# Attention scores of two heads on 64 rows each instead of stacked on 128 rows

## The chip, the cores and the metric

One core of a Trainium2 chip runs the whole program. The metric is the device time of one execution in microseconds (us); lower is better. The names of the engines are those of the profile: PE is TensorE (matmuls, with PEld for its weight loads), DVE is VectorE, ACT is ScalarE, POOL is GpSimd, SP is SyncE, which issues the DMAs.

## What is computed

The reference is a decoder trunk of two layers over 512 tokens of width 1024, in float32. Each layer is a half-step SwiGLU, a token mixer, and a second half-step SwiGLU, each modulated by vectors of c and closed by a post-norm:

```python
for l in range(DEPTH):                                   # DEPTH = 2
    y = _swiglu(_modulate(x, sh1, sc1), ...);  x = _post_norm(x, y, g1, FFN_RES, ...)
    y = _token_mixer(_modulate(x, sh2, sc2), w_in[l], w_out[l]);  x = _post_norm(x, y, g2, 1.0, ...)
    y = _swiglu(_modulate(x, sh3, sc3), ...);  x = _post_norm(x, y, g3, FFN_RES, ...)
```

The change is in the token mixer. It projects its input to ten blocks and runs three groups of four heads: retention, dilated softmax attention, and stick-breaking attention. Two of them need scores of queries with keys over a head width of 64:

```python
z  = einsum('bhqd,bhsd->bhqs', q_blk * d**-0.5, k)       # stick-breaking, no positions, strictly causal
sc = einsum('bhqd,bhqpjd->bhqpj', q_blk * d**-0.5, k_g)  # dilated windows, q and k rotated before
```

The kernel computes the dilated scores against all keys of the causal range and adds the logarithm of how often a pattern holds each key.

## The kernel before

**Split products.** A matrix product of two float32 operands is made of float32r parts: each operand is split into an upper part `hi` and the rest `lo`, and PE adds up hi·hi, hi·lo and lo·hi in PSUM (`mm3`, L180 to L183). For weights, `unit` (L167) loads a piece of 512 KB into a raw tile, ACT writes `hi` (L176), DVE writes `lo` (L177). The products of the projections are the lines L181, L182, L183 in every table.

**The mixer.** `mixer` (L504) first makes the projections `sv` and `sq`. The other projections are generators (`jobs`). The attentions (`stick` L675, `dilated` L740, `retention` L788) are generators too: at each `yield` they hand over a number of microseconds of PE work, which `fill` takes from the projections and puts in between. So the order on PE is a score product, some projection products, the next dependent product of an attention, and so on. A scheduler fixes the final order of each engine before the program runs, and every engine then works through its own list in that order.

**Heads by pairs.** The projections of q and k come out transposed, [128, 512 tokens] for a pair of heads: head a = 0 stands in rows 0 to 63, head a = 1 in rows 64 to 127 (`hsl(a)`). Before, `stack_q` and `stack_k` make a stacked copy of 128 rows for each head: for q, the upper part on the head's own 64 rows and the lower part on the other 64; for k, the upper part on both halves, and the lower parts in a tile of their own (`sklo`, `dklo`). One product over 128 rows then gives hi·hi + hi·lo of one head, and one product over 64 rows gives lo·hi. A score call (`scores_T` for stick, `scores_q` for dilated) makes four matmuls: full, 64 rows, full, 64 rows (L615 and L616, L628 and L629), with a PSUM bank per head. There are 8 calls per attention and layer, with 256, 256, 384 and 512 columns for each of the two pairs.

**Stick-breaking.** A step takes the scores, makes `sb_w` (absolute value, exp, log on ACT: L700, L703, L704), `sb_sp` (DVE L706, POOL L708), its parts `sb_hi` (ACT L711) and `sb_lo` (DVE L712). PE sums those over the keys (L722, L723 for the block itself; L727, L728 for later blocks). The scores of step n + 1 are issued on PE between the scores of step n and L722 of step n.

**Dilated.** The scores are scaled and masked (DVE L750), the maximum is taken (L752), exp on ACT (L755), the division on DVE (L756, L758) into `d_sc`; PE transposes it (L770), ACT copies it out (L773), PE multiplies it with the values (L780). The scores of step n + 1 stand ahead of the transposes of step n.

**Rotation.** q and k of the dilated heads go through `rotate` (L643) ahead of the stacking: four copies on ACT (L650), DVE L651, POOL L652, DVE L653.

Of the kernel before, what the change touches and what calls it, by code (L numbers as in the profile page):

```python
# [10 lines left out]
F32 = mybir.dt.float32  # L11
F32R = mybir.dt.float32r
# [4 lines left out]
P = 128  # L17
D = 1024
T = 512
# [48 lines left out]
def trunk(ctx: ExitStack, tc: tile.TileContext, x_in, c_in, w_ada, b_ada, ln_gain, ln_bias,  # L68
# [18 lines left out]
    def big(shape, dt=F32, name="big"):  # L87
        return bigp.tile(shape, dt, tag="big", name=name)
# [145 lines left out]
    def chain(parts):  # L234
        """The steps of several vectors; what follows a sum over the partitions comes a few steps behind it."""
        u, late = [], None
        for steps, final in parts:
            if late is None:
                u += steps
            else:  # L240
                u += steps[:POST] + [late] + steps[POST:]
            late = final
        return u + [lambda: None] * POST + [late] if parts else u
# [51 lines left out]
    class PostNorm:  # L295
# [59 lines left out]
        def head(self):  # L355
            """The first token pair's part of the next input."""
            if self.h is not None:
                make_h(0, self.h, self.a, self.b)

        def rest(self):  # L360
            """The second token pair's part of the next input, and the residual stream."""
            ends = make_h(1, self.h, self.a, self.b)
            with tc.issue_after(self.last.ins):
                for t in range(NT):
                    G.tensor_tensor(out=xres[t], in0=xres[t], in1=self.gain, op=ALU.mult)
                    G.tensor_tensor(out=xres[t], in0=xres[t], in1=self.bias, op=ALU.add)
            return ends

# [28 lines left out]
    def gu_units(l, wg, wu, f, n, spare=False):  # L397
        """Units of gate and up for ff tiles f .. f+n-1, as (which, first k, units)."""
        us = []
        kn = 8 // n  # L400
        for wi, w in enumerate((wg, wu)):
            for k0 in range(0, KC, kn):
                us.append((wi, k0, kn, unit(w[l, k0 * P:(k0 + kn) * P, f * P:(f + n) * P]
                                            .rearrange("(k p) f -> p k f", p=P), (kn, n * P), spare)))
        return us

    REST_AT = 3       # unit of the first group after which the second token pair's input is made
    REST_AT_Q = 3     # the same in the mixer, by row chunks of the first projection
    LAST_CUT = (256, 256, 512, 1024)  # columns that VectorE finishes at the end, per token tile
    DRAIN = (3, 2)    # adaLN steps per group of gate and up, and per unit of down  # L410
    RES = 4           # units of down that stay for the token-major end
    ACT_HEADS = (1, 3)  # retention heads whose norm ScalarE applies
    OUT_EARLY = 2     # token tiles of the output projection begun beside retention
    # projections, in us of the tensor engine, put between the dependent parts of the attentions
# [62 lines left out]
    def hsl(a):  # L477
        return slice(a * HD, (a + 1) * HD)
# [4 lines left out]
    def pair_psum(N):  # L483
        """PSUM for two [P, N] blocks: views per block, and one view of both when they share a bank."""
        if fits(N):
            ps = psum()
            v = ps[:, 0:2 * N].rearrange("p (a n) -> p a n", a=2)
            return [v[:, 0, :], v[:, 1, :]], [(slice(0, 2), v)]
        b = [psum(), psum()]
        return [b[0][:, 0:N], b[1][:, 0:N]], [(a, b[a][:, 0:N]) for a in range(2)]  # L490

    class Packs:
        """[P, 2, N] tiles for N = 128, 256, 384, 512: 128 and 384 share a slot."""
# [10 lines left out]
    def mixer(l, h, pre, rest, prefetch, nxt):  # L504
        hh, hl = h
        yT = {}
        # -- projections, as generators that yield the time of what they gave to the tensor engine --
# [62 lines left out]
        def stack_q(name, m, src, scale=1.0):  # L570
            """[P, 2, T]: per head its rows' upper and lower parts, one part at the head's own rows."""
            r = big([P, 2, T], F32R, name)
            for a in range(2):
                o, x = hsl(a), hsl(1 - a)
                S.activation(out=r[o, a, :], in_=src[o, :], func=AF.Copy, scale=scale)
                V.scalar_tensor_tensor(out=r[x, a, :], in0=src[o, :], scalar=scale, in1=r[o, a, :].bitcast(F32),
                                       op0=ALU.mult, op1=ALU.subtract)
            val[name, m] = r

        def stack_k(name, m, src):  # L580
            """Per head its rows' upper parts twice, and the lower parts at the head's own rows."""
            r = big([P, 2, T], F32R, name)
            if m == 0:
                val[name, "lo"] = big([P, 2, T], F32R, name + "lo")
            lo = val[name, "lo"]
            for a in range(2):
                o, x = hsl(a), hsl(1 - a)
                S.copy(out=r[o, a, :], in_=src[o, :])
                V.tensor_copy(out=r[x, a, :], in_=r[o, a, :].bitcast(F32))
                V.tensor_tensor(out=lo[o, m, :], in0=src[o, :], in1=r[o, a, :].bitcast(F32), op=ALU.subtract)  # L590
            val[name, m] = r
# [7 lines left out]
        def wide(lo, hi):  # L599
            """At least 256 columns, the wanted ones within them."""  # L600
# [5 lines left out]

        def scores_T(kn, qn, pr, J):
            """Per head of pair pr, in banks apart: [keys of block J, queries >= 128 J]."""
            cs, v = wide(J * P, T)
            res = []  # L610
            for a in range(2):
                ps = psum()
                w = ps[:, 0:cs.stop - cs.start]
                js = slice(J * P, (J + 1) * P)
                PE.matmul(w, lhsT=val[kn, pr][:, a, js], rhs=val[qn, pr][:, a, cs], start=True, stop=False)  # L615
                PE.matmul(w, lhsT=val[kn, "lo"][hsl(a), pr, js], rhs=val[qn, pr][hsl(a), a, cs], start=False, stop=True)  # L616
                res.append(ps[:, v])
            return res

        def scores_q(qn, kn, pr, i):  # L620
            """Per head of pair pr, in banks apart: [queries of block i, keys < 128 (i + 1)]."""
            cs, v = wide(0, (i + 1) * P)
            res = []
            for a in range(2):
                ps = psum()
                w = ps[:, 0:cs.stop - cs.start]
                js = slice(i * P, (i + 1) * P)
                PE.matmul(w, lhsT=val[qn, pr][:, a, js], rhs=val[kn, pr][:, a, cs], start=True, stop=False)  # L628
                PE.matmul(w, lhsT=val[qn, pr][hsl(a), a, js], rhs=val[kn, "lo"][hsl(a), pr, cs], start=False, stop=True)  # L629
                res.append(ps[:, v])  # L630
            return res
# [42 lines left out]
        # -- stick-breaking heads, weights as [keys, queries] --  # L674
# [64 lines left out]
        # -- dilated heads: one softmax over the keys, each counted as often as a pattern holds it --  # L739
# [45 lines left out]
        # -- retention heads --  # L785
# [128 lines left out]
        # -- first projections: tokens of the first pair before those of the second --  # L914
# [11 lines left out]
        keep_T("sq", lambda name, m, src: stack_q(name, m, src, QK_SCALE))(ps_q)  # L926
# [10 lines left out]
        def job_decay():  # L937
# [4 lines left out]
            ("sk", job_T("sk", keep_T("sk", stack_k))),  # L942
            ("dtab", job_tables(("dtab", rope_t[1].rearrange("a p t -> p a t")))),
            ("dv", job_tok("dv", keep_tok("dv"))),
            ("dq", job_T("dq", rotate("dq", "dtab", stack_q))),
            ("dk", job_T("dk", rotate("dk", "dtab", stack_k))),
# [61 lines left out]
    def startup():  # L1008
# [6 lines left out]
        def sums(k):  # L1015
            """Chunk k of shift and scale, summed over the rows that share a partition; loads of chunk k."""
# [72 lines left out]
    def vectors(l, s):  # L1089
        """The vectors worked out beside sub-layer s of layer l."""  # L1090
# [58 lines left out]
```

## Time and profile before

| | |
|---|---|
| three timed runs | 2039.39, 2039.91, 2044.3 us; median 2039.91 |
| span of the profiled execution, from its first to its last instruction | 2038.1 us |
| PE busy | 1975.2 us, 97% of the span |
| DVE, ACT, POOL busy | 1172.5, 698.5, 375.9 us |
[...]
| DMA | 263.13 MB, mean 129 GB/s |

What lies around the span is 1.8 us when the median is taken. "Busy" counts an engine's own instructions. The end of a matmul is modelled in the profile, and matmuls overlap in it, so the time that one takes from PE is read from its start to the start of the next. The two mixers lie at about 390 to 665 us and 1395 to 1670 us of the span; stick-breaking fills 438 to 530 us in the first, the dilated heads 530 to 588 us.

### The profile page before, as it was taken

To read this page: it belongs to the slowest core of one execution; us is meant where nothing else is said; L and a number is where in the kernel's file an instruction comes from. 1 tells how busy PE (TensorE), PEld (TensorE's weight loads), DVE (VectorE), ACT (ScalarE), POOL (GpSimd) and SP (SyncE) were. 2 spreads that over 40 slices of the span, in tenths; PEclk is the share of its full clock that TensorE was granted. 3 is DMA by queue.
4 is the path that set the end of the run, shared out by engine and by line. 5 is a ranking of instruction groups with operands and counts; after the bars stand their busy time and mean duration, and the time that the engine had idled before them with its cause. 6 is when DMAs were issued, how large, how long until landed. Compare 5 with 4: busy or idle time off the path is not lost.

```text
span 2038.1 us, 24729 instructions
## 1 busy us (share of the span) xinstructions
PE 1975.2 (97%) x9920; PEld 1649.4 (81%) x9920; DVE 1172.5 (58%) x1497; ACT 698.5 (34%) x971; POOL 375.9 (18%) x236
## 2 busy tenths in 40 slices
PE   7999999999999899999989999999999989999997
PEld 5888887887888788878878888888887878888886
DVE  8655566676567745564495555328665686333325
ACT  3323212357543322322233222224665432322211
POOL 5011123142221401112041102104222032000002
PEclk9999999999999899999999999999999999999999
DMA  9555566332212555555335555422321226333221
GB/s 290 178 165 155 154 205 224 120 103 69 70 53 83 155 155 156 157 182 177 104 120 162 158 149 166 154 93 83 105 80 58 85 71 184 95 94 103 93 95 60
DMA packets 177931, 263.13 MB, mean 129 GB/s; under 512 B 8602, under 2 KB 144274, under 8 KB 177816
## 3 DMA queue, kind: packets, MB, share of 16 engines
q1 hardware_dynamic: 177816, 261.55, 42.1%
q8 instruction: 78, 1.28, 0.3%
q14 instruction: 37, 0.30, 0.0%
HBM read 259.42 MB, written 2.10 MB: 128 GB/s over the span
## 4 chain that ended last, share of the span: by engine, by line
PE 60%; issue 18%; DVE 10%; DMA 6%; POOL 3%; ACT 2%; SPq 1%; DVEq 0%; POOLq 0%; ACTq 0%
PE ps L181 15%; PE ps L183 15%; PE ps L182 15%; DMA raw<-in_w_ada_dram 4%; PE ps L376 3%; PE ps L379 3%; PE ps L375 3%; DVE acc L202 2%; DVE lo L177 2%; POOL red L206 1%; DVE st L315 1%; DVE xall L313 1%; PE ps L275 1%; DMA raw<-in_ffn_w_down_dram 1%; DVE hT_lo L286 1%
## 5 line engine op out<-in xcount | busy, mean ns | idle before, releaser
L177 DVE TENSOR_TENSOR lo<-raw,hi 128x1024 fp32r<-128x1024 f32 (+1 forms) x302 | 443.3, 1473 | 432.5 <-ACT hi L176 432.0
L181 PE MATMUL ps<-hT_hi,hi 128*128 128x512 f32 x1472 | 574.1, 392 | 4.9 <-ACT hT_hi L1064 4.9
L176 ACT CAST hi<-raw 128x1024 fp32r<-128x1024 f32 (+1 forms) x302 | 314.9, 1046 | 763.8 <-PE ps L182 347.4
L182 PE MATMUL ps<-hT_lo,hi 128*128 128x512 f32 x1472 | 574.1, 390 | 0.1
L183 PE MATMUL ps<-hT_hi,lo 128*128 128x512 f32 x1472 | 573.6, 390 | 0.0
L181 PEld LDWEIGHTS ps<-hT_hi,hi 128*128 128x128 f32 x1472 | 276.3, 188 | 65.0 <-ACT hT_hi L1064 6.5
L183 PEld LDWEIGHTS ps<-hT_hi,lo 128*128 128x128 f32 x1472 | 276.7, 188 | 57.8
L182 PEld LDWEIGHTS ps<-hT_lo,hi 128*128 128x128 f32 x1472 | 276.9, 188 | 57.5 <-DVE hT_lo L1065 1.1
L202 DVE SCALAR_TENSOR_TENSOR acc<-raw,cond,acc 128x1024 f32<-128x1024 f32 x118 | 172.3, 1460 | 185.2 <-DMA raw<-in_w_ada_dram 179.9
L376 PE MATMUL ps<-lo,gT 128*128 128x512 f32 x576 | 225.1, 391 | 3.9 <-DVE lo L177 3.9
L375 PE MATMUL ps<-hi,gT 128*128 128x512 f32 x576 | 225.1, 391 | 3.3 <-DVE sg L392 3.3
L206 POOL PARTITION_ALL_REDUCE red<-acc x16 | 100.4, 6274 | 622.7 <-DVE acc L202 622.7
L379 PE MATMUL ps<-hi,gT 128*128 128x512 f32 x576 | 178.0, 390 | 0.0
L376 PEld LDWEIGHTS ps<-lo,gT 128*128 128x128 f32 x576 | 108.5, 188 | 28.0 <-DVE lo L177 5.6
L375 PEld LDWEIGHTS ps<-hi,gT 128*128 128x128 f32 x576 | 108.6, 188 | 26.6 <-DVE sg L392 4.1
L146 POOL TENSOR_TENSOR rstd<-rstd,mhalf 128x1 f32<-128x1 f32 x24 | 15.5, 644 | 620.5 <-DVE rstd L145 617.8
L379 PEld LDWEIGHTS ps<-hi,gT 128*128 128x128 f32 x576 | 108.4, 188 | 22.7
L391 ACT ACTIVATE sg<-ps 128x512 f32<-128x512 f32 x88 | 51.6, 592 | 161.7 <-PE ps L183 161.7
L181 PE MATMUL ps<-hi,hT_hi 128*128 128x256 f32 x320 | 93.9, 293 | 0.0
L182 PE MATMUL ps<-lo,hT_hi 128*128 128x256 f32 x320 | 90.4, 283 | 0.0
L183 PE MATMUL ps<-hi,hT_lo 128*128 128x256 f32 x320 | 90.4, 282 | 0.0
L393 ACT CAST gT<-sg 128x512 fp32r<-128x512 f32 x88 | 52.9, 620 | 63.1 <-DVE sg L392 62.8
(406 smaller groups left out, 2599.5 us busy)
## 6 DMA issues: line engine op xcount, KB each, us to landing
raw<-in_w_ada_dram SPq DMA_DIRECT2D x128, 512.0 KB, 3.7
raw<-in_ffn_w_down_dram SPq DMA_DIRECT2D x88, 512.0 KB, 3.5
raw<-in_ffn_w_gate_dram SPq DMA_DIRECT2D x85, 512.0 KB, 3.8
raw<-in_ffn_w_up_dram SPq DMA_DIRECT2D x85, 512.0 KB, 3.9
raw<-in_w_in_dram SPq DMA_DIRECT2D x48, 512.0 KB, 3.6
ada<-in_w_ada_dram SPq DMA_DIRECT2D x32, 256.0 KB, 5.2
raw<-in_w_out_dram SPq DMA_DIRECT2D x16, 512.0 KB, 3.5
bcrow<-in_ln_gain_dram SPq DMA_DIRECT2D x6, 512.0 KB, 5.4
```

What stands on the lines that cost most here:

```text
L176: S.copy(out=hi, in_=raw)
L177: mods["dve"] = V.tensor_tensor(out=lo, in0=raw, in1=hi.bitcast(F32), op=ALU.subtract)
L181: PE.matmul(dst, lhsT=sh, rhs=mh, start=first, stop=False)
L182: PE.matmul(dst, lhsT=sh, rhs=ml, start=False, stop=False)
L183: return PE.matmul(dst, lhsT=sl, rhs=mh, start=False, stop=last)
L202: mods["dve"] = V.scalar_tensor_tensor(out=acc, in0=raw, scalar=cond[:, k:k + 1], in1=acc, op0=ALU.mult, op1=ALU.add)
L206: G.partition_all_reduce(st["red"], st["acc"], P, bass_isa.ReduceOp.add)
L375: PE.matmul(ps2[hf], lhsT=sh, rhs=wh[:, cs], start=first, stop=False)
L376: PE.matmul(ps2[hf], lhsT=sh, rhs=wl[:, cs], start=False, stop=False)
L379: PE.matmul(ps2[hf], lhsT=sl, rhs=wh[:, cs], start=False, stop=last)
L391: S.activation(out=sg, in_=ps_g, func=AF.Silu)
L393: S.copy(out=g[:, 0, :], in_=sg)
```

## The change

`stack_q` and `stack_k` go; `halves` takes their place for `sq`, `sk`, `dq` and `dk`. It keeps the upper parts of both heads of a pair in one plane of 128 rows and the lower parts in a second plane, with one ACT and one DVE instruction over all 128 rows. The two score functions call a common one, which makes three products over 64 rows for each head, and alternates the heads: six matmuls, with both banks taken at the start. The three products are the same as before. The diff also drops comments and docstrings, which moves the line numbers; that part is left out here.

```diff
-        def stack_q(name, m, src, scale=1.0):
-            r = big([P, 2, T], F32R, name)
-            for a in range(2):
-                o, x = hsl(a), hsl(1 - a)
-                S.activation(out=r[o, a, :], in_=src[o, :], func=AF.Copy, scale=scale)
-                V.scalar_tensor_tensor(out=r[x, a, :], in0=src[o, :], scalar=scale, in1=r[o, a, :].bitcast(F32),
-                                       op0=ALU.mult, op1=ALU.subtract)
-            val[name, m] = r
-
-        def stack_k(name, m, src):
-            r = big([P, 2, T], F32R, name)
-            if m == 0:
-                val[name, "lo"] = big([P, 2, T], F32R, name + "lo")
-            lo = val[name, "lo"]
-            for a in range(2):
-                o, x = hsl(a), hsl(1 - a)
-                S.copy(out=r[o, a, :], in_=src[o, :])
-                V.tensor_copy(out=r[x, a, :], in_=r[o, a, :].bitcast(F32))
-                V.tensor_tensor(out=lo[o, m, :], in0=src[o, :], in1=r[o, a, :].bitcast(F32), op=ALU.subtract)
-            val[name, m] = r
+        def halves(name, m, src, scale=1.0):
+            r = big([P, 2, T], F32R, name)
+            S.activation(out=r[:, 0, :], in_=src, func=AF.Copy, scale=scale)
+            V.scalar_tensor_tensor(out=r[:, 1, :], in0=src, scalar=scale, in1=r[:, 0, :].bitcast(F32),
+                                   op0=ALU.mult, op1=ALU.subtract)
+            val[name, m] = r
...
+        def scores(pr, fixed, js, moved, cs, v):
+            x, y = val[fixed, pr], val[moved, pr]
+            ps = [psum() for _ in range(2)]
+            for n, (i, j) in enumerate(((0, 0), (0, 1), (1, 0))):
+                for a in range(2):
+                    PE.matmul(ps[a][:, 0:cs.stop - cs.start], lhsT=x[hsl(a), i, js], rhs=y[hsl(a), j, cs],
+                              start=(n == 0), stop=(n == 2))
+            return [p[:, v] for p in ps]
+
         def scores_T(kn, qn, pr, J):
-            cs, v = wide(J * P, T)
-            res = []
-            for a in range(2):
-                ps = psum()
-                w = ps[:, 0:cs.stop - cs.start]
-                js = slice(J * P, (J + 1) * P)
-                PE.matmul(w, lhsT=val[kn, pr][:, a, js], rhs=val[qn, pr][:, a, cs], start=True, stop=False)
-                PE.matmul(w, lhsT=val[kn, "lo"][hsl(a), pr, js], rhs=val[qn, pr][hsl(a), a, cs], start=False, stop=True)
-                res.append(ps[:, v])
-            return res
+            return scores(pr, kn, slice(J * P, (J + 1) * P), qn, *wide(J * P, T))
...
```

`scores_q` changes in the same way. The order on the engines, at two places:

On PE, the scores of the third stick step of the first layer (384 columns), before. The names are the output, then the moving and the stationary operand.

```order
L183 MATMUL ps_3262<-hi_3177,hT_lo_2694 128x256
L615 MATMUL ps_3417<-sq_3148,sk_3232 128x384
L616 MATMUL ps_3417<-sq_3148,sklo_3233 128x384
L615 MATMUL ps_3420<-sq_3148,sk_3232 128x384
L616 MATMUL ps_3420<-sq_3148,sklo_3233 128x384
L181 MATMUL ps_3436<-hT_hi_2693,hi_3250 128x512
```

The same place after the change:

```order
L183 MATMUL ps_3249<-hi_3173,hT_lo_2694 128x256
L599 MATMUL ps_3408<-sq_3148,sk_3228 128x384
L599 MATMUL ps_3409<-sq_3148,sk_3228 128x384
L599 MATMUL ps_3408<-sq_3148,sk_3228 128x384
L599 MATMUL ps_3409<-sq_3148,sk_3228 128x384
L599 MATMUL ps_3408<-sq_3148,sk_3228 128x384
L599 MATMUL ps_3409<-sq_3148,sk_3228 128x384
L181 MATMUL ps_3429<-hT_hi_2693,hi_3237 128x512
```

Four matmuls become six, which stand together and alternate between the two banks. What stands around them on PE is the same, here and at the other calls.

On DVE, the preparation of `dk` within the second half of stick-breaking, before (the rows from the rotation of the first pair to the second pair's):

```order
L653 TENSOR_TENSOR rot_3698<-rot_3698,rtmp_3697 128x512
L177 TENSOR_TENSOR lo_3742<-raw_3740,hi_3741 128x1024
L589 CAST dk_3706<-dk_3706 64x512
L590 TENSOR_TENSOR dklo_3707<-rot_3698,dk_3706 64x512
L589 CAST dk_3706<-dk_3706 64x512
L590 TENSOR_TENSOR dklo_3707<-rot_3698,dk_3706 64x512
L651 TENSOR_TENSOR rot_3715<-ps_3596,dtab_3247 128x512
```

The same place after the change:

```order
L631 TENSOR_TENSOR rot_3693<-rot_3693,rtmp_3692 128x512
L177 TENSOR_TENSOR lo_3728<-raw_3726,hi_3727 128x1024
L574 SCALAR_TENSOR_TENSOR dk_3701<-rot_3693,dk_3701 128x512
L629 TENSOR_TENSOR rot_3705<-ps_3587,dtab_3234 128x512
```

Four DVE instructions between the two rotations become one.

## Rows read from the trace of the kernel before

**Rows 1.** The page, part 1: busy time of each engine over the span.
```profile
PE 1975.2 (97%) x9920; PEld 1649.4 (81%) x9920; DVE 1172.5 (58%) x1497; ACT 698.5 (34%) x971; POOL 375.9 (18%) x236
```

**Rows 2.** Windows: length, PE, PEld, DVE, ACT, POOL busy, clock, DMA share, GB/s.
```profile
438.00:530.00 92.00, 90.83 (x557) 77.02 (x556) 60.16 (x93) 61.32 (x95) 21.12 (x36) 1.00 0.24 76
530.00:588.00 58.00, 58.00 (x385) 46.57 (x383) 31.23 (x59) 34.39 (x72) 13.94 (x10) 1.00 0.20 62
```

**Rows 3.** A 64-row score line: duration ns min/median/max, first and last start, forms.
```profile
L616 PE MATMUL ps<-sq,sklo x32: 379/410/498, 439.4 to 1511.3; 64*128 64x256 f32 x16, 64*128 64x384 f32 x8, 64*128 64x512 f32 x8
```

**Rows 4.** Timeline of PE, a stick call of 256 columns: start us, duration us.
```profile
443.25 0.28 PE L183 MATMUL ps<-hi,hT_lo 128*128 128x256 f32 x1
443.37 0.28 PE L615 MATMUL ps<-sq,sk 128*128 128x256 f32 x1
443.58 0.38 PE L616 MATMUL ps<-sq,sklo 64*128 64x256 f32 x1
443.89 0.39 PE L615 MATMUL ps<-sq,sk 128*128 128x256 f32 x1
444.21 0.38 PE L616 MATMUL ps<-sq,sklo 64*128 64x256 f32 x1
444.52 0.39 PE L181 MATMUL ps<-hi,hT_hi 128*128 128x256 f32 x1
```

**Rows 5.** The same view, ends of a stick call of 512 columns.
```profile
461.26 0.39 PE L183 MATMUL ps<-hT_hi,lo 128*128 128x512 f32 x1
461.48 0.39 PE L615 MATMUL ps<-sq,sk 128*128 128x512 f32 x1
461.80 0.50 PE L616 MATMUL ps<-sq,sklo 64*128 64x512 f32 x1
...
463.07 0.50 PE L181 MATMUL ps<-hT_hi,hi 128*128 128x512 f32 x1
```

**Rows 6.** The same view, ends of a dilated call of 256 columns.
```profile
530.26 0.39 PE L628 MATMUL ps<-dk,dq 128*128 128x256 f32 x1
...
531.51 0.50 PE L181 MATMUL ps<-hT_hi,hi 128*128 128x512 f32 x1
```

**Rows 7.** The same view, retention: full-height transposes, then matmuls on alternating 64 rows (two, all).
```profile
588.62 0.71 PE L804 MATMUL ps<-ident,rk 128*128 128x128 f32 x5
...
589.05 0.27 PE L804 MATMUL ps<-ident,rk 128*128 128x128 f32 x1
589.25 0.38 PE L818 MATMUL ps<-rq,rk 64*128 64x128 f32 x2
...
589.25 2.06 PE L818 MATMUL ps<-rq,rk 64*128 64x128 f32 x32
```

**Rows 8.** The same view, sixth stick step; in brackets idle time and releaser.
```profile
500.78 0.28 PE L183 MATMUL ps<-hi,hT_lo 128*128 128x256 f32 x1
501.89 0.38 PE L722 MATMUL ps<-sb_hi,uneg 128*128 128x256 f32 x1 [0.83 <-ACT sb_hi L711]
502.62 0.39 PE L723 MATMUL ps<-sb_lo,uneg 128*128 128x256 f32 x1 [0.34 <-DVE sb_lo L712]
```

**Rows 9.** Timeline of ACT and DVE ahead of it: start us, busy us.
```profile
489.05 1.26 ACT L588 CAST dk<-rot 64x512 fp32r<-64x512 f32 x2
...
491.69 1.79 DVE L590 TENSOR_TENSOR dklo<-rot,dk 64x512 fp32r<-64x512 f32 x1
...
495.04 1.26 ACT L588 CAST dk<-rot 64x512 fp32r<-64x512 f32 x2 [3.53 <-DVE rot L653]
```

**Rows 10.** Timeline of DVE and PE at two transposes of the dilated heads.
```profile
535.32 0.47 DVE L758 TENSOR_SCALAR d_sc<-d_sc,d_den 128x128 f32<-128x128 f32 x2
536.10 0.38 PE L770 MATMUL ps<-ident,d_sc 128*128 128x128 f32 x2
...
568.71 0.61 DVE L758 TENSOR_SCALAR d_sc<-d_sc,d_den 128x256 f32<-128x256 f32 x2
570.39 0.60 PE L770 MATMUL ps<-ident,d_sc 128*128 128x128 f32 x4
```

More of the change, by code (lines that the diff above doesn't have):

```diff
@@ L605, in wide @@
             return slice(lo, lo + 256), slice(0, hi - lo)
-        def scores_T(kn, qn, pr, J):
-            cs, v = wide(J * P, T)
-            res = []
-            for a in range(2):
-                ps = psum()
-                w = ps[:, 0:cs.stop - cs.start]
-                js = slice(J * P, (J + 1) * P)
-                PE.matmul(w, lhsT=val[kn, pr][:, a, js], rhs=val[qn, pr][:, a, cs], start=True, stop=False)
-                PE.matmul(w, lhsT=val[kn, "lo"][hsl(a), pr, js], rhs=val[qn, pr][hsl(a), a, cs], start=False, stop=True)
-                res.append(ps[:, v])
-            return res
-        def scores_q(qn, kn, pr, i):
[L622 to L631, printed above, removed]
+        def scores(pr, fixed, js, moved, cs, v):
[6 more added lines that the diff above has]
+            return [p[:, v] for p in ps]
+        def scores_T(kn, qn, pr, J):
+            return scores(pr, kn, slice(J * P, (J + 1) * P), qn, *wide(J * P, T))
+        def scores_q(qn, kn, pr, i):
+            return scores(pr, qn, slice(i * P, (i + 1) * P), kn, *wide(0, (i + 1) * P))
         def tok_to(name, op):
@@ L925, in mixer @@
                 ps_v.append(psum())
-        keep_T("sq", lambda name, m, src: stack_q(name, m, src, QK_SCALE))(ps_q)
+        keep_T("sq", lambda name, m, src: halves(name, m, src, QK_SCALE))(ps_q)
         def job_tables(*names):
@@ L941, in mixer @@
         jobs.extend([
-            ("sk", job_T("sk", keep_T("sk", stack_k))),
+            ("sk", job_T("sk", keep_T("sk", halves))),
             ("dtab", job_tables(("dtab", rope_t[1].rearrange("a p t -> p a t")))),
             ("dv", job_tok("dv", keep_tok("dv"))),
-            ("dq", job_T("dq", rotate("dq", "dtab", stack_q))),
-            ("dk", job_T("dk", rotate("dk", "dtab", stack_k))),
+            ("dq", job_T("dq", rotate("dq", "dtab", halves))),
+            ("dk", job_T("dk", rotate("dk", "dtab", halves))),
             ("logc", job_logc()),
```

## The prediction, made blind

> **What bounds the kernel now.** I read the busy shares first: PE works for 97% of the span [rows 1]. Then the stretches where the changed instructions stand. In the stick stretch PE is busy for 90.83 of 92 us, in the dilated one for all of 58 us, at full granted clock, while DVE and ACT are busy for about two thirds and half [rows 2]. So here a microsecond that PE doesn't need is a microsecond of the span, unless the chain over ACT, DVE and POOL then comes last. What counts is therefore the time from the start of the first score matmul to the start of whatever follows, and then the waits on that chain. Each score line has 32 matmuls, 16 of 256 columns, 8 of 384 and 8 of 512 [rows 3]; with two per call that is 32 calls, 16 stick and 16 dilated.
>
> **What a call costs before.** A stick call of 256 columns runs from 443.37 to 444.52, 1.15 us for four matmuls, while the full matmul ahead of it takes 0.12 us of the stream [rows 4]. Each change between 128 and 64 rows shows: the full matmul in front of a 64-row one takes 0.21 instead of 0.12 (0.09 until the array is free), and the 64-row one takes 0.31 (0.11 more, its weights loaded in the open, then 0.12, then 0.09 before the next change). With 512 columns the stream takes 0.22 to 0.23 per matmul and the call 1.59 us [rows 5]. 384 columns lie in the middle, 1.37. A dilated call of 256 columns takes 1.25 us [rows 6], 0.10 more, since the matmul in front has another shape (the values, 64 columns wide), so that its first matmul pays for a change as well; I add the same 0.10 to the others, 1.47 and 1.69. One dilated call per layer follows a full matmul and costs the 1.15 of a stick call.
>
> **What a call costs after.** Six matmuls over 64 rows, in three pairs. Retention already issues 64-row matmuls of the two heads in turn, and its rows give the price of a pair. Five full-height transposes of 128 columns take 0.109 us each (588.62 to 589.05). The first two L818 matmuls together span 0.38 us from 589.25, about what a single one spans behind a change of shape, so they start within 0.01 us of each other. All 32 end at 591.31, and the last pair starts about 0.27 earlier (the span of a single one without a change), at 591.04: 1.79 us for 15 pairs, that is 0.21 for the first (0.11 of it weights, as above) and 0.113 for each of the 14 that follow [rows 7]. So two matmuls on different halves of the array take what one full matmul takes, each with its own weight load hidden. These are float32, the scores float32r; I take the rate of a pair as that of one full float32r matmul, 0.12, 0.175 and 0.23 us for the three widths. A call then costs 0.11 for the first weights, three pairs, and 0.09 at the end: 0.56, 0.725, 0.89. Stick calls pay 0.09 in front as well (0.65, 0.815, 0.98); dilated calls paid for that change before.
>
> **The sum on PE.** Saved per stick call: 1.15 − 0.65 = 0.50, 1.37 − 0.815 = 0.555, 1.59 − 0.98 = 0.61. Per layer 4 × 0.50 + 2 × 0.555 + 2 × 0.61 = 4.3 us. Per dilated call: 0.69, 0.745, 0.80, and 0.50 for the one behind a full matmul; per layer 3 × 0.69 + 0.50 + 2 × 0.745 + 2 × 0.80 = 5.7 us. Two layers: **20.0 us**. The bounds: if the two heads run one after the other, the three pairs cost six matmuls. Then a stick call costs 1.01, 1.34, 1.67 (saves 0.14, 0.03, −0.08) and a dilated one 0.92, 1.25, 1.58 (saves 0.33, 0.22, 0.11, and 0.14 once); per layer 0.5 + 1.8, in all 4.5 us. On the other side, without any cost for the changes of shape, the 32 calls save up to 32 × 0.2 = 6 us more. I take 20.0, as the L818 rows are the nearest operation, and the bounds only for the range.
>
> **The preparation.** For each of sq, sk, dq, dk and each pair, two ACT instructions of 0.58 to 0.63 us become one, and two (q) or four (k) DVE instructions become one. Nearly all of that stands beside PE work and costs nothing now, with one exception. In the sixth stick step PE stands still for L722 and then L723: 501.89 − 500.78 = 1.11 where the stream takes 0.12, and 0.73 until L723 where two such matmuls stand 0.17 apart, about 1.55 us per layer [rows 8]. Behind it stands a queue: DVE is in the stacking of dk until 493.48, the rotation of the second pair comes behind that, ACT waits for it 3.53 us until 495.04, and only then makes sb_w of this step [rows 9]. With one instruction in place of four, that DVE stretch ends about 2.6 us earlier; ACT's and POOL's parts of the rotation hold it to about 2 us, and ACT's own stack at 495.04 saves another 0.6. So sb_lo is ready some 2.5 us earlier, while PE comes 0.55 us earlier (the 384 call in between), and the chain is no longer late: **3.1 us** in two layers. Bounds: nothing of it (the chain stays as late as PE comes early), to all.
>
> **A new wait.** The scores of step n + 1 stand between the scores of step n and what uses them, so PE now comes to each use 0.5 to 0.9 us earlier. At the first transposes of the dilated heads the division ends at 535.79, PE comes at 536.10: 0.31 us to spare [rows 10]. PE will come 0.50 (second call) + 0.69 (first call) = 1.2 us earlier, the chain about 0.7, as both heads' scores are ready when PE leaves the call. That leaves a wait of roughly 0.35 us per layer, between 0 and 0.9; I count **−0.7 us** in two layers. The tightest of the other dilated steps has 570.39 − 569.32 = 1.07 us to spare, against 0.75 to 0.8 [rows 10], the others more, so they stay free. Behind a waiting L770 on PE stand the projections' matmuls, which nobody waits for there.
>
> 20.0 + 3.1 − 0.7 = 22.4 us off the span of 2038.1, that is 2015.7. The median of the runs shown lies 1.8 above the span, so the forecast is 2039.9 − 22.4 = **2017.5 us**.
>
> **Rivals.**
>
> *The weights come into the open.* If the load for a half can't run while that half is computing, each pair after a call's first shows 0.11 more: 32 × 2 × 0.11 = 7.0 us, so 2024.5. Against it: L818 at 0.113 per pair, and as many PEld as PE records beside it [rows 2, 7]. For it: nothing in float32r shows a pair. [...]
>
> *The chains take it.* If in all dilated steps with a next call PE waits for what that call saved (7 × 0.7 × 2 = 10 us) the time is about 2028. For it: the 0.31 us. Against it: the other slack.
>
> *The heads run one after the other,* so that the change doesn't give what "side by side" says: 4.5 + 3.1 = 7.6 us, 2032.3. It needs the 0.01 us between the L818 starts not to hold for these.
>
> *Slower: every change of half costs what a change of shape costs.* Then each of the six matmuls takes what L616 takes, 0.31 (256), 0.365 (384), 0.42 (512), each the spacing of its width and 0.19 [rows 4], plus 0.09 in front for stick. Stick calls lose 0.80, 0.91, 1.02, dilated ones 0.61, 0.72, 0.83 (0.80 once): per layer 7.1 + 5.7, in all 25.6 slower, less 3.1, about 2062. It decides from 7.6 / (32 × 5) = 0.05 us per change of half. L818 changes half 31 times without it [rows 7].
>
> **How the numbers follow.** The forecast with its small terms (2013 to 2021) 0.74; weights in the open 0.10; chains 0.06; one after the other 0.05; slower 0.03; 0.02 for no change by something that I don't see. About 0.3%, 6 us, is what a measurement of this kernel tells from no change. All cases but the last two lie below 2033.8: faster 0.95, same 0.02, slower 0.03. The range reaches from 2012 (the changes of shape cost less than counted) to 2026, past the open weights.
>
> **What would show it.** Right: in the changed trace the two heads' matmuls start within 0.01 us of each other, pairs 0.12 apart at 256 columns and 0.23 at 512, a stick call of 256 columns is over in 0.56 us; L722's wait in the sixth step is gone; the transposes of the first dilated step wait about 0.35 us. Wrong: pairs 0.24 or 0.34 apart (one after the other; weights in the open would show 0.23), more waits of PE before the transposes, or PE idle elsewhere in the mixers.

## The result, and the profile after

The changed kernel takes 2018.7 us (median of 4 runs, 2012.6 to 2021.28), the kernel before 2039.65 beside it (4 runs, 2037.12 to 2044.3). The ratio is 0.989, with a 95% interval of 0.9869 to 0.9912. The forecast was 2017.5. The profiled run took 2018.21 us with a span of 2016.5.

The page of the changed kernel, busy time of each engine; it answers to [rows 1]:

```profile
PE 1956.5 (97%) x9984; PEld 1642.8 (81%) x9984; DVE 1149.9 (57%) x1465; ACT 689.3 (34%) x955; POOL 377.1 (19%) x236
```

There are 64 more matmuls (32 calls with six in place of four), and yet PE is busy for 18.7 us less. The span is best divided at the places that the change touches. One stretch per layer runs from the first score matmul of stick-breaking to the last product with the values in the dilated heads. Here are windows of the kernel before, each with its length, the busy time of PE, PEld, DVE, ACT and POOL with their instructions, the granted clock, the DMA share and GB/s. The first is the first stretch (the second, from 1442.85, takes 149.12), the other is what lies between the two, below called the middle.

```profile
439.20:588.24 149.04, 147.87 (x933) 122.63 (x932) 90.22 (x150) 94.50 (x166) 35.06 (x46) 1.00 0.22 69
...
588.24:1442.85 854.61, 834.70 (x4065) 701.57 (x4061) 498.48 (x571) 254.62 (x319) 154.67 (x58) 0.99 0.46 139
```

The same windows of the changed kernel:

```profile
436.06:573.52 137.46, 137.37 (x965) 118.19 (x964) 81.67 (x137) 90.59 (x160) 35.02 (x46) 1.00 0.23 75
...
573.52:1433.46 859.94, 838.97 (x4066) 705.34 (x4062) 496.04 (x568) 253.89 (x317) 154.59 (x58) 0.99 0.43 139
```

The second stretch takes 137.44. Each is 11.6 to 11.7 us shorter, 23.3 in all; the prediction had 22.4. PE's idle time in it fell from 1.17 us to 0.09. Outside, the start was 3.1 us shorter in this profile, the middle 5.3 longer and the end 0.5 shorter, which makes the 21.6 us between the two spans. What belongs to the run in that is said below.

A stick call of 256 columns on PE, the same one as [rows 4]. The columns are start us and duration us. x2, x4 and x6 count the instructions that a line groups, from the start of the first to the end of the last: the call's first two, all six, the last four and the last two.

```profile
439.46 0.28 PE L183 MATMUL ps<-hi,hT_lo 128*128 128x256 f32 x1
439.67 0.39 PE L599 MATMUL ps<-sq,sk 64*128 64x256 f32 x2
...
439.67 0.62 PE L599 MATMUL ps<-sq,sk 64*128 64x256 f32 x6
440.22 0.39 PE L181 MATMUL ps<-hi,hT_hi 128*128 128x256 f32 x1
...
439.89 0.40 PE L599 MATMUL ps<-sq,sk 64*128 64x256 f32 x4
...
440.01 0.28 PE L599 MATMUL ps<-sq,sk 64*128 64x256 f32 x2
```

The first two matmuls together span 0.39, about what a single one spans behind a change of shape [rows 4], so they start together. The second pair starts 0.22 behind the first and the third 0.12 behind the second; the call is over in 0.55 us, from 439.67 to 440.22. In front of it lie 0.21, 0.09 more than the stream's 0.12, as the prediction counted for stick calls. A call of 512 columns in stick-breaking, beside [rows 5]:

```profile
456.72 0.97 PE L599 MATMUL ps<-sq,sk 64*128 64x512 f32 x6
457.62 0.50 PE L181 MATMUL ps<-hT_hi,hi 128*128 128x512 f32 x1
```

It takes 0.90 us; those in the dilated heads take 0.89 to 0.91. All 32 calls together take 21.75 us (43.4 before). Less the 0.09 in front of the 18 that follow a full matmul, the calls gave 20.0 us. What stands around them on PE is not the same everywhere: before, the first stick call of each layer lay in three places among the projections' matmuls (439.19, 440.77, 441.52), and now it stands together. It paid the 0.09 once more there, in each layer, which brings the calls to 20.2.

The sixth stick step, which answers to [rows 8], and the chain ahead of it on DVE, which answers to [rows 9]:

```profile
493.70 0.28 PE L183 MATMUL ps<-hi,hT_lo 128*128 128x256 f32 x1
493.82 0.28 PE L700 MATMUL ps<-sb_hi,uneg 128*128 128x256 f32 x1
493.94 0.28 PE L701 MATMUL ps<-sb_lo,uneg 128*128 128x256 f32 x1
```

```profile
483.74 0.68 DVE L574 SCALAR_TENSOR_TENSOR dk<-rot,dk 128x512 fp32r<-128x512 f32 x1
...
492.73 0.69 DVE L690 TENSOR_TENSOR sb_lo<-sb_sp,sb_hi 128x512 fp32r<-128x512 f32 x1 [1.34 <-ACT sb_hi L689]
```

The stream runs through at 0.12 per matmul: sb_lo ends at 493.42, half a microsecond before L701 starts. One DVE instruction of 0.68 stands where four stood, and the second rotation starts 0.18 behind it, at 484.60.

The transposes of the dilated heads, which answer to [rows 10], on PE, then on DVE and POOL:

```profile
525.37 0.40 PE L182 MATMUL ps<-hT_lo,hi 128*128 128x512 f32 x1
525.60 0.28 PE L748 MATMUL ps<-ident,d_sc 128*128 128x128 f32 x1
525.63 0.48 PE L183 MATMUL ps<-hT_hi,lo 128*128 128x512 f32 x1
525.95 0.27 PE L748 MATMUL ps<-ident,d_sc 128*128 128x128 f32 x1
...
556.10 0.28 PE L183 MATMUL ps<-hi,hT_lo 128*128 128x256 f32 x1
556.47 0.63 PE L748 MATMUL ps<-ident,d_sc 128*128 128x128 f32 x4
```

```profile
555.31 1.28 DVE L736 TENSOR_SCALAR d_sc<-d_sc,d_den 128x256 f32<-128x256 f32 x2
```

```profile
554.19 1.98 POOL L778 TENSOR_TENSOR r_qx<-rq,decay 128x384 f32<-128x384 f32 x2 [0.80 <-issue]
```

In the first step the two transposes no longer stand together in PE's list: a projection's matmul lies between them, and the first starts 0.23 behind the 512 columns in front of it, which is the stream. In the sixth step the transposes come 0.37 behind a matmul of 256 columns, a wait of 0.25 us. There the two divisions take 1.28 us, where two of this size took 0.61 in the kernel before [rows 10], and POOL is at work on r_qx at the same time (554.19 to 556.17). In the kernel before POOL did the same after the divisions:

```profile
571.08 2.00 POOL L800 TENSOR_TENSOR r_qx<-rq,decay 128x384 f32<-128x384 f32 x2 [4.99 <-PE ps L770]
```

The other traces agree. A single division of 128x256 takes 1.00 to 1.03 us wherever r_qx runs beside it (in the repetition, with the heads apart and with the load of dk back), and 0.34 to 0.36 everywhere else.

### The profile page after: what moved, and what is told of

It reads as the page before. It is cut to its first block, busy times and chain, and to the rows that moved or that the text cites. A ratio compares the mean times of both kernels' runs of the same rounds, so it can differ in the third digit from the quotient of the medians.

```text
span 2016.5 us, 24796 instructions
## 1 busy us (share of the span) xinstructions
PE 1956.5 (97%) x9984; PEld 1642.8 (81%) x9984; DVE 1149.9 (57%) x1465; ACT 689.3 (34%) x955; POOL 377.1 (19%) x236
## 3 DMA queue, kind: packets, MB, share of 16 engines
q8 instruction: 78, 1.28, 0.2%
## 4 chain that ended last, share of the span: by engine, by line
PE 64%; issue 17%; DVE 8%; DMA 6%; ACT 2%; POOL 1%; SPq 1%; DVEq 0%; POOLq 0%; ACTq 0%
PE ps L181 16%; PE ps L182 15%; PE ps L183 15%; PE ps L376 4%; PE ps L379 4%; PE ps L375 4%; DMA raw<-in_w_ada_dram 3%; DVE acc L202 2%; DVE lo L177 1%; PE ps L599 1%; DMA raw<-in_ffn_w_down_dram 1%; DVE st L315 1%; DVE xall L313 1%; PE ps L275 1%; DMA raw<-in_ffn_w_up_dram 1%
## 5 line engine op out<-in xcount | busy, mean ns | idle before, releaser
L392 DVE TENSOR_TENSOR sg<-sg,ps 128x512 f32<-128x512 f32 x88 | 57.4, 682 | 28.6 <-PE ps L183 28.6
```

What stands on the lines that cost most here:

```text
L392: V.tensor_tensor(out=sg, in0=sg, in1=ps_u, op=ALU.mult)
```

## The experiments

**Heads apart.** Is it the order, the two heads side by side, that gives the half price? In `scores` the loops are exchanged:

```
-            for n, (i, j) in enumerate(((0, 0), (0, 1), (1, 0))):
-                for a in range(2):
+            for a in range(2):
+                for n, (i, j) in enumerate(((0, 0), (0, 1), (1, 0))):
```

> The changed kernel with the six score matmuls of a call in another order: the three of head 0, then the three of head 1; everything else as changed. Theory (matmuls on the two halves run together only where they stand side by side, and PE starts them in order): only the last of head 0 and the first of head 1 meet, so a call takes five steps of the stream in place of three. A dilated call of 256 columns takes 0.79 us instead of 0.55, one of 512 about 1.35 instead of 0.89; over the 32 calls 10.3 us more PE time, about 2029. Rival A (the halves never run together, the gain came from fewer changes of shape): no difference to the changed kernel, a call stays at 0.55. Rival B (PE pairs them by itself in any order): the same, 0.55, but with starts of the two heads in pairs. Rival C (no overlap at all in this order): six steps, 0.91 us for 256 columns, 15.5 us more, about 2034.

2023.96 us (2019.13 to 2024.99), ratio to the kernel before 0.9899, interval 0.9885 to 0.9912 (changed kernel on the same chip below: 0.989, 0.9876 to 0.9903). PE's list has three matmuls of head 0, then three of head 1:

```
L599 MATMUL ps_3262<-sq_3148,sk_3228 128x256 x3
L599 MATMUL ps_3263<-sq_3148,sk_3228 128x256 x3
```

The timeline of a stick call on PE, and one wait in the dilated heads:

```profile
442.02 0.39 PE L599 MATMUL ps<-sq,sk 64*128 64x256 f32 x2
...
442.02 0.63 PE L599 MATMUL ps<-sq,sk 64*128 64x256 f32 x6
442.58 0.39 PE L181 MATMUL ps<-hi,hT_hi 128*128 128x256 f32 x1
...
563.04 0.66 PE L758 MATMUL ps<-d_pt,dv 128*64 128x128 f32 x8 [0.46 <-ACT d_pt L751]
```

The call takes 0.56 us against 0.55 in the changed kernel, and its records start in pairs, 0.01 apart, though the two of a pair stand three places apart in the list. All calls together take 21.94 us against 21.75. So the theory that the matmuls must be issued alternately is wrong for these six: it was enough here that the other half's first stood three places behind. The records don't name the half; that a pair is one of each head is concluded from the time, since a half alone takes 0.12 us for each of its matmuls, as the last experiment with two steps shows. The stretch is 138.26 us, 0.8 longer, 0.46 of it the wait shown; for the whole kernel the two orders can't be told apart.

**Stacked, regrouped.** Is it the full-height product and the stacked copies, or only the changes of shape, that cost? The kernel before, with the four matmuls of a call in another order, in `scores_T` and `scores_q`:

```
+            ps = [psum() for _ in range(2)]
...
             for a in range(2):
-                ps = psum()
...
+                PE.matmul(ws[a], ..., start=True, stop=False)
+            for a in range(2):
+                PE.matmul(ws[a], ..., start=False, stop=True)
```

The first of the two runs over 128 rows, the second over 64.

> The kernel before with its stacked copies, but the four matmuls of a call in another order, with both banks taken first: the two full ones, then the two 64-row ones side by side. Theory: on PE two full matmuls and one pair cost the same stream as three pairs, with one change of shape in and one out, so a stick call of 256 columns takes 0.12 + 0.21 + 0.31 = 0.64 us from its first start, against 1.15 before and 0.09 + 0.55 in the changed kernel; nearly all of the 20 us comes without the new copies. The preparation is that of before, so the wait at L722 and L723 of the sixth stick step stays, 1.5 to 2.2 us per layer since PE comes earlier: 3 to 4.5 us slower than the changed kernel, about 2022. Rival A (the gain comes from the lighter preparation on DVE and ACT): time like before, 2039. Rival B (the wait was no matter of the stacking): no wait there and the time of the changed kernel, 2018.7.

2033.47 us (2030.53 to 2034.83), ratio 0.9949, 0.9935 to 0.9962: faster than before, 12 us slower than the changed kernel on the same chip, and 11 slower than expected. The timeline of a stick call and of the sixth stick step on PE:

```profile
442.33 0.40 PE L614 MATMUL ps<-sq,sk 128*128 128x256 f32 x2
442.66 0.39 PE L616 MATMUL ps<-sq,sklo 64*128 64x256 f32 x2
442.97 0.39 PE L181 MATMUL ps<-hi,hT_hi 128*128 128x256 f32 x1
...
496.68 0.28 PE L183 MATMUL ps<-hi,hT_lo 128*128 128x256 f32 x1
499.27 0.58 PE L720 MATMUL ps<-sb_hi,uneg 128*128 128x256 f32 x1 [2.31 <-ACT sb_hi L709]
499.99 0.58 PE L721 MATMUL ps<-sb_lo,uneg 128*128 128x256 f32 x1
```

Its windows: the first stretch, two of 2 us from the sixth step on, and the sixth step of the second layer:

```profile
438.16:583.30 145.14, 142.69 (x933) 121.80 (x932) 89.83 (x150) 94.57 (x166) 35.83 (x46) 0.98 0.23 71
...
499.00:501.00 2.00, 1.59 (x5) 1.30 (x6) 0.69 (x1) 1.97 (x5) 0.00 (x0) 0.50 0.00 0
...
505.00:507.00 2.00, 2.00 (x14) 1.64 (x12) 2.00 (x5) 1.37 (x2) 0.52 (x2) 0.79 0.69 240
...
1498.00:1508.00 10.00, 7.35 (x42) 6.34 (x41) 6.09 (x13) 7.45 (x12) 2.62 (x6) 0.83 0.14 44
```

A stick call of 256 columns takes 0.64 us instead of 1.15 with the same four matmuls, and that is what the change makes of it with six (0.55 and 0.09 in front). The two 64-row matmuls start together here too. In the dilated heads a call takes 0.75 (256) to 1.09 us (512), since the change from the values' 64 columns and the change to 64 rows both remain. The first stick call of each layer still lies spread among the projections' matmuls, as before. All calls together take 27.4 us: 16.0 less than before, where the change saves 20.0.

Yet the two stretches are only 9.0 us shorter (289.17 against 298.16). The rest went at the sixth step. PE comes there earlier and the stacking of dk is as late as ever, so PE stands still for 2.31 us; until L721 the wait is (499.27 − 496.68 − 0.12) + (0.72 − 0.17) = 3.0 us instead of 1.55, so 1.5 more. And the granted clock, 1.00 until then, falls to 0.50, the lower level, until about 505.8: the projections' matmuls of 256 columns stand 0.21 apart instead of 0.12. Of some 6 us of work at that level 0.09 in 0.21 is lost, 2.6 us. In the second layer the clock is at 0.83 over 1498 to 1508, which makes 3.4 us at the lower level and a loss of 1.5. These are estimates, and they add up: 16.0 − 2 × 1.5 − 2.6 − 1.5 = 8.9. So the two halves of the change need each other: faster calls alone run into the chain of dk, and pay for it twice, with the wait and with the clock. DVE and POOL ahead of it:

```profile
487.96 0.68 DVE L590 TENSOR_TENSOR dklo<-rot,dk 64x512 fp32r<-64x512 f32 x1
489.09 1.79 DVE L590 TENSOR_TENSOR dklo<-rot,dk 64x512 fp32r<-64x512 f32 x1
```

```profile
489.03 1.30 POOL L650 TENSOR_TENSOR rtmp<-rtmp,dtab 128x512 f32<-128x512 f32 x1 [3.40 <-ACT rtmp L648]
```

The second of two equal DVE instructions takes 1.1 us more while POOL's instruction runs. So did its like in the kernel before [rows 9], beside a POOL instruction of 1.29 us that began at 491.65.

**Load of dk back.** The wait at the sixth step by itself: the changed kernel, and for dk the DVE and ACT work of the old stacking again, or nearly, into a tile that nothing reads.

```
+            if name == "dk":
+                xt = big([P, 2, T], F32, "dkx")
+                S.copy(out=xt[hsl(0), 1, :], in_=src[hsl(0), :])
+                V.tensor_copy(out=xt[hsl(0), 0, :], in_=xt[hsl(0), 1, :])
+                V.tensor_copy(out=xt[hsl(1), 0, :], in_=src[hsl(1), :])
+                V.tensor_tensor(out=xt[hsl(1), 1, :], in0=src[hsl(1), :], ..., op=ALU.subtract)
             val[name, m] = r
```

> The changed kernel with the load of the old preparation of dk put back: beside the two new instructions, one more copy of 64 rows on ACT and three more 64-row instructions on DVE for each pair, into a tile that nobody reads. The scores and all else as changed. Theory (the preparation of dk is ahead of the sixth stick step on ACT and DVE, and PE now comes earlier than before): PE's calls stay at 0.55 us, but the wait ahead of the sums of the sixth step comes back, 2 to 3.3 us per layer, larger than the 1.55 of before; the attention stretch grows from 137.4 to 140 or 141 us, in all 4 to 6.5 us slower than the changed kernel, about 2026 on this chip. Rival (the missing wait is owed to the earlier scores alone, not to the preparation): no wait there, stretch 137.4, time as changed.

2022.19 us (2021.94 to 2025.49) beside 2041.96 for the kernel before on that chip: ratio 0.9907, 0.989 to 0.9924. The sixth step on PE:

```profile
497.05 0.28 PE L183 MATMUL ps<-hi,hT_lo 128*128 128x256 f32 x1
497.56 0.38 PE L706 MATMUL ps<-sb_hi,uneg 128*128 128x256 f32 x1 [0.23 <-ACT sb_hi L695]
498.28 0.39 PE L707 MATMUL ps<-sb_lo,uneg 128*128 128x256 f32 x1 [0.34 <-DVE sb_lo L696]
```

```profile
439.41:577.98 138.57, 137.91 (x965) 118.33 (x964) 84.78 (x143) 91.51 (x162) 36.19 (x46) 1.00 0.23 74
```

The wait is back, with nothing changed on PE: 0.39 us before L706 and 0.61 before L707 beyond the stream, together half of the least that was expected. The stretch is 1.12 us longer than in the changed kernel, 2.2 in both layers, where the prediction gave the removal of the wait 3.1. The DVE instructions of the preparation take 0.69 us at most here; none of them is drawn out beside POOL's. The total can't be told from the changed kernel's. So the preparation is enough to cause the wait. That its size hangs on whether DVE and POOL meet fits both kernels, but no run tests it alone.

**Two steps.** If the changes of shape at the two ends of a call are all that is left to save, calls put together in twos should be cheaper still.

```
             z(0)
+            z(1)
...
-                if n + 1 < len(steps):
+                if n % 2 == 1 and n + 1 < len(steps):
                     z(n + 1)
+                    z(n + 2)
```

and in the same way for the dilated scores.

> The changed kernel with the score calls of two steps issued together (steps 0 and 1, then 2 and 3, ...), in both attentions: 16 groups of twelve matmuls instead of 32 groups of six; the same products and the same fillers. Theory (each group pays once: 0.09 in front where a full matmul stands there, 0.11 for the first weights, 0.09 at the end): 8 stick groups fewer save 0.29 each, 8 dilated ones 0.20 each, 3.9 us, about 2015; the transposes of odd steps have more time, those of even steps less. Rival (the chains over ACT and DVE take it back, since both steps' work now comes at once and in the even steps nothing stands between scores and their use): PE time per score falls by the same 3.9 us, but waits at the transposes or at the sums of the stick steps return as much or more, 2018 to 2022.

2019.69 us (2018.22 to 2020.86), ratio 0.9882, 0.9869 to 0.9896. Two calls of 256 columns, and the first stretch:

```profile
440.27 0.98 PE L599 MATMUL ps<-sq,sk 64*128 64x256 f32 x12
441.18 0.39 PE L181 MATMUL ps<-hi,hT_hi 128*128 128x256 f32 x1
```

```profile
440.27:576.18 135.91, 135.47 (x965) 118.51 (x964) 79.59 (x137) 90.17 (x160) 33.63 (x46) 1.00 0.24 75
```

0.91 us for two calls instead of 2 × 0.55 + 0.09, and the stretch is 1.5 us shorter in each layer, 3.1 in all where the theory had 3.9. A part is given back: in small waits behind the softmax, the two largest 0.5 and 0.4 us over both layers, and in one group per layer (531.21), where head 1 of the second call starts late and the group takes 1.71 us instead of the 1.42 of its like. Between whole kernels, 2019.69 and 2021.64, the intervals overlap: the gain is seen in the stretch, not shown in the time.

**Two steps, heads apart.** How far ahead may the other half's matmuls stand? Twelve matmuls, six of head 0 and then six of head 1.

```
+            for a in range(2):
+                for p, (pr, fixed, js, moved, cs, v) in zip(ps, calls):
...
+                    for n, (i, j) in enumerate(((0, 0), (0, 1), (1, 0))):
+                        PE.matmul(p[a]...)
```

> The kernel of the joint calls (two steps together) with the twelve matmuls of a group in the order: all six of head 0, then all six of head 1. It asks how far ahead PE starts the other half's matmuls. Theory A (each half works through its own matmuls, however they are issued, as the run with three and three showed): starts in pairs 0.01 us apart, a group of 2 x 256 columns takes 0.91 us as in the joint calls, the stretch stays at 136 us. Theory B (PE looks only a few matmuls ahead): head 1 starts late, the group takes up to 0.11 + 11 x 0.12 + 0.09 = 1.5 us, and the stretch grows by up to 5 us per layer.

One run: 2019.39 us, span 2017.7. The first two calls on PE, and at their end the last two matmuls and the last one:

```profile
438.54 0.50 PE L598 MATMUL ps<-sq,sk 64*128 64x256 f32 x2
...
438.54 1.33 PE L598 MATMUL ps<-sq,sk 64*128 64x256 f32 x12
439.80 0.39 PE L181 MATMUL ps<-hi,hT_hi 128*128 128x256 f32 x1
...
439.47 0.40 PE L598 MATMUL ps<-sq,sk 64*128 64x256 f32 x2
...
439.59 0.28 PE L598 MATMUL ps<-sq,sk 64*128 64x256 f32 x1
```

1.26 us, between 0.91 (alternating) and the 1.5 of twelve in a row. The first two together span 0.50 us, where with the heads apart in threes they spanned 0.39: the second starts 0.22 behind the first. The first pair comes 0.34 us in, the third matmul with the fourth (0.341 and 0.348). Read so, head 1 starts once head 0's third has started, with three of head 0 still waiting. All 16 groups show it, at 0.34 us where the first call has 256 columns and at 0.46 where it has 384. The program has head 1's first matmul in this group wait for nothing later than a matmul some hundred places ahead, so it is the order that holds it back. So head 1 started here past three waiting matmuls of head 0 but not past four or five, and the order matters. At the end, where only head 1 is left, the matmuls stand 0.12 us apart one by one: a half alone takes for one matmul what the two halves take for a pair. That the halves work at the same time, and not that a matmul of 64 rows is quicker, is thereby shown. And the loss is seen: the stretch is 138.20 us, 2.3 longer than with the alternating order.

**The changed kernel again,** on the chip of "Heads apart", "Stacked, regrouped" and "Two steps".

> The changed kernel once more, beside the others on one chip: 2018.7 again, 21 us under the kernel before; a reading that the gain was the draw of one run would have it move by some us towards 2039.

2021.64 us (2018.14 to 2023.43), before 2043.33 (9 runs): ratio 0.989, 0.9876 to 0.9903. The start and the first stretch:

```profile
0.00:439.89 439.89, 413.62 (x1937) 342.42 (x1938) 275.54 (x329) 132.28 (x166) 101.89 (x59) 1.00 0.60 181
439.89:577.34 137.45, 137.35 (x964) 118.20 (x964) 81.60 (x137) 90.81 (x160) 35.03 (x46) 1.00 0.24 75
```

The stretch repeats within 0.01 us, while the start takes 3.8 us more than in the first profile of the same kernel. The start thus differs by as much between two profiles of one kernel as the first profile had less than before, 3.1 us; that part is no gain of the change.

## Why the prediction came out right

The forecast was 1.2 us off the median. By its terms:

- **The calls on PE, 20.0 us: 20.0 measured,** 20.2 with the first calls, which stood apart before. The prices were taken from retention's L818 [rows 7]. Calls were put at 0.56, 0.725 and 0.89 us and took 0.55, 0.72 and 0.90. That float32r pairs run like float32 pairs was the open step; it held: a pair of 256 columns takes 0.12 us, as one full float32r matmul does.
- **The wait of the sixth stick step, 3.1 us: gone.** That the preparation is enough for it is shown by bringing that load back: 2.2 of the 3.1 return. The remaining 0.9 would fit the DVE instruction of 1.79 us beside POOL in [rows 9], which the load brought back didn't meet; that part is argued, not shown.
- **The new wait, −0.7 us: 0.25 per layer, at another place.** The prediction put 0.35 at the first transposes and said that the other dilated steps stay free. The first transposes don't wait: the scheduler drew a projection's matmul between the two, so that only one division had to be over. The sixth step waits instead, as DVE's divisions took 1.28 in place of 0.61 us. The prediction counted the slack of that step with the DVE time of before; r_qx on POOL now came earlier and ran beside the divisions. So this step of the prediction failed, and the sum of the term is nearly right by accident.
- 20.2 + 3.1 − 0.5 = 22.8 of the 23.3 us in the two stretches. 0.5 are not assigned.
- **The time gained, 21.0 us by the medians, is 2.3 less than the stretches gave.** The middle of the span is 5.3 us longer in the changed profile, with the same instructions and most of it as PE busy time. In the repetition it is 861.35 us (577.34 to 1438.69), with the heads apart 856.17, with two steps 860.44, in the one profile of before 854.61. The granted clock accounts for most of it. In the middle PE works 8.8 us at the lower level (granted clock 0.50) in the kernel before, 18.7 in the changed one, 20.6 in its repetition and 10.1 with the heads apart. With half of that taken off, an estimate (at 0.50, matmuls of 512 columns start 0.43 us apart behind 896.92 in the changed kernel, and 0.23 to 0.24 apart at 1.00 behind 899.60), its busy time is 830.3, 829.6, 829.3 and 830.5 us, nearly the same. One of these places in the changed kernel, behind a wait of 3.00 us for DVE that ended at 895.15:

```profile
895.79:899.20 3.41, 3.41 (x10) 2.66 (x9) 2.84 (x4) 1.04 (x1) 0.00 (x0) 0.50 0.79 256
```

The kernel with the heads apart has hardly more of it than the kernel before, so it is no fixed price of the change. Whether the change brings it about more often is open: side by side on one chip, the mean granted clock is 0.989 in four runs of the changed kernel and 0.991 in nine of the kernel before.

- **The total is partly luck.** The stretches gave 0.9 us more than the 22.4 of the forecast, the middle took 5.3 back, and in the profile the start and the end gave 3.6. None of the last three was in the sum.

The rivals: weights in the open (0.11 more for each pair after the first, so 0.23 between the second and the third) are refuted, these stand 0.12 apart at 256 columns. A price for each change of half is refuted by the same rows, and one head after the other by the pairs; exchanging the loops did not bring it either. The chains took little of it: PE is idle for 0.09 us in the whole stretch, where that rival has 5. The prediction took it from the change that the heads must be issued side by side; for six matmuls that isn't so, and nothing of its sum hung on it.

The prediction put the 0.11 behind a change of shape down to a weight load in the open, and the 0.09 in front to the array not being free. Here is the first stick call of the kernel before, weight loads and matmuls:

```profile
439.08 0.19 PEld L615 LDWEIGHTS ps<-sq,sk 128*128 128x128 f32 x1
439.19 0.28 PE L615 MATMUL ps<-sq,sk 128*128 128x256 f32 x1
439.40 0.18 PEld L616 LDWEIGHTS ps<-sq,sklo 64*128 64x128 f32 x1
439.40 0.38 PE L616 MATMUL ps<-sq,sklo 64*128 64x256 f32 x1
```

The load of the full matmul starts 0.11 ahead of its matmul, that of the 64-row one together with its matmul, which lasts 0.10 longer. That the array has to be free first is the author's reading of the 0.09; the rows show that this load starts 0.21 behind the start of the full matmul, not what it waits for.

## What to carry to other kernels

Where a matmul needs only 64 rows, two of them on the two halves cost here what one full matmul costs (0.12 us at 256 columns), so three products per head in 64 rows are cheaper here than two that alternate between 128 and 64 rows (0.55 us a call against 1.15). Each change of shape costs about 0.2 us here (0.09 in front and 0.11 behind), so put matmuls of one shape together first: that alone brought the same four matmuls from 1.15 to 0.64 us. Price such an edit from rows of the same kernel that already do it. Before counting on a faster tensor engine, look for the chain that it will run into: with the stacked copies kept, regrouping gave only about 10 us of 22.

## What the runs showed of the hardware beyond that

- Matmuls for the two halves did not have to alternate here. With three of one half ahead, those of the other start beside them (0.01 us behind); with six ahead, they start with the third (0.34 us in, one run, all 16 groups).
- A DVE instruction of 64 x 512 float32 took 0.68 us alone and 1.79 beside a POOL instruction of 1.30 us which began 0.06 us earlier. POOL's ended at 490.33 and DVE's at 490.88, 0.55 later, a little less than the 0.68 that it takes alone; an estimate from these is that some 0.13 us of its work was done while POOL's ran. A division on DVE (128x256, one tensor and a scalar per row) took 1.00 to 1.03 us beside POOL's r_qx and 0.34 to 0.36 otherwise.
- After 2.31 us of idle time in the regrouped kernel PE's granted clock was 0.50 for 6.8 us in the first layer, from before the work went on. In the second layer, after 2.31 us of idle time at the same step, it fell 1.5 us after the work had gone on, and for 3.4 us. Around the wait of 0.83 us in [rows 8] it stayed at 1.00 [rows 2]. So here the idle time was followed by a loss beyond itself, and the same idle time not by the same one: 2.6 and 1.5 us by the estimates above.
